# Decode attention, memory attention and retention of a hybrid layer computed in 32-wide tiles of the matmul array

## The chip, the core and the metric

One Trainium2 chip, one of its cores, one launch of one program. The metric is the device time of that launch in microseconds (us), the median over several runs; the profile is one further execution with the profiler on. Six units are named below: TensorE (PE for its matmuls, PEld for its weight loads), VectorE (DVE), ScalarE (ACT), GpSimd (POOL), SyncE (SP), which issues every transfer of this kernel, and the 16 DMA engines.

## The reference

One step of a layer with three gated branches. It is computed for a prompt of 2048 tokens and for 8 decode sequences of 16 new tokens each; "decode" below means the latter.

```python
h = rms_norm(x, g_norm);  z = h @ w_in                       # 1024 -> 9224
fq, fk, fv, ff, fg, rq, rk, rv, rg, mq, mg, gl = split_proj(z)
# A: 8 heads x 64; decode: 16 queries against 2048 cached keys and 16 new ones
s = q.k * 64**-0.5 + c_q - c_k;  p = softmax(s, causal);  fox_o = p @ v
# B: 4 heads, key width 128, value width 256; decode starts from a given state S
o     = (q @ S) * dec_q + ((q @ k.T) * dmask) @ v
S_new = gamma**L * S + (k * dec_k).T @ v
# M: 4 heads x 128 against 256 memory tokens
mem_o = softmax(mq @ mk.T * 128**-0.5) @ mv
y = x + (sum_i gate_i * (branch_i * silu(g_i)) @ w_p_i) @ w_out
```

All arrays are float32. The caches of A for decode hold 8 x 2048 x 512 keys and as many values.

## The kernel before, in words

The program has three stages. The first makes the projections for all tokens and stores them in DRAM (to about 1690 us). The second runs two lanes that a helper `weave` interleaves: the right lane does retention (prompt tiles, then `sample` for the decode sequences) and then `fox`, the prompt's attention of branch A; the left lane does the forget gates, `mem_prompt`, `decode_mem`, `decode_fox`, and then, when decode is finished and its buffers are given back, `out_block` for the first two token tiles (merge and output projection). The third stage is the other `out_block` calls. The order in which each engine gets its instructions is set when the program is built, by a scheduler that follows its own estimate of times; on the chip each engine then works through its list in that order.

Matmuls are written `T.matmul(out, stationary, moving)`. Type F32R is a reduced form, and a float32 value is split into two of them (`hi` and `lo`), with two or three matmuls; type F32 is used whole. In the trace a whole-F32 matmul shows as two weight loads and two matmuls, here called two passes, and an F32R matmul as one.

The steps that the change touches:

- `decode_fox`, `unit(b)`, one sequence. A column of the score bank `sc` (128 rows) is head group x 16 queries. `qblk` holds, for each of 4 head pairs `g`, a 128 x 128 stationary in which all columns but 32 are zero, so that four F32 matmuls of 128 columns over 512 keys add up in one bank (L1460); L1461 adds the forget term from 16 rows `crow`. A fifth, short chunk takes the 16 new keys (L1466 to L1468). Row maximum on DVE, exp on ACT; two units are in flight.
- Values: the probabilities are transposed (L1487) and split into hi and lo, which stand side by side as one 128-column stationary `dpr`; each value tile `dvt` is split too, by ACT (L1497, `dvh`) and POOL (L1499, `dvl`); then four F32R matmuls of 256 moving columns for each 128 keys (L1504). Only the blocks that belong to a head pair are used of the 128 x 512 result; L1520 sums hi and lo and transposes, by matmuls with `sumid`.
- `decode_mem`: the same with 4 heads, 64 columns and F32 (L1611, L1628, with transposes L1622 and L1635).
- `sample` in retention: for each of two head pairs and each sequence `b`, the states come in 256 KB loads `st0`, the queries of `b` are copied into a zeroed block `zq` (name qz), the keys are masked for `b` into `zk` (name kz); F32 matmuls L1188 (output) and L1189 (new state).
- `softmax_scale`, used by both `fox` and `decode_fox`: a subtraction on DVE and one exp on ACT (L1222, L1223).

Of the kernel before, what the change touches and what calls it, by code (L numbers as in the profile page):

```python
# [72 lines left out]
def body(ctx: ExitStack, tc: tile.TileContext, a, o, stop=99):  # L73
# [1019 lines left out]
    def retention(rp, rw):  # L1093
# [58 lines left out]
        def sample():  # L1152
# [7 lines left out]
            zq = rw.tile([P, 2, 2, P], F32, name="qz", bufs=1)  # L1160
            G.memset(zq, 0.0)
            yield
            ob = rw.tile([P, 4, 256], F32, name="ob", bufs=OB)
            for h2 in range(2):
# [5 lines left out]
                if h2:  # L1170
                    for b in (NB - 2, NB - 1):
                        G.memset(zq[:, b % 2, :, b * TS:(b + 1) * TS], 0.0)
                for b in range(NB):
                    bs = slice(b * TS, (b + 1) * TS)
                    s0 = rw.tile([P, 2, 256], F32, name="st0", bufs=3)
                    dma(s0, a["state_ret"][b][hs].rearrange("h k v -> k h v"))
                    zb = zq[:, b % 2]
                    if b >= 2:
                        G.memset(zb[:, :, (b - 2) * TS:(b - 1) * TS], 0.0)
                    G.tensor_copy(zb[:, :, bs], qt.rearrange("p (h l) -> p h l", h=4)[:, hs, bs])  # L1180
                    zk = rw.tile([P, 256], F32, name="kz")
                    G.tensor_scalar(zk, k[:, h2 * 256:(h2 + 1) * 256], kc[:, K_BM + b:K_BM + b + 1], 1.0, ALU.mult, ALU.mult)
                    up = prm()
                    sn = rw.tile([P, 2, 256], F32, name="sn0")
                    for i in range(2):
                        h = 2 * h2 + i
                        oc = slice(i * 256, (i + 1) * 256)
                        T.matmul(op[:, oc], zb[:, i], s0[:, i], start=False, stop=b == NB - 1 and i == 1)  # L1188
                        T.matmul(up[:, oc], zk[:, i * P:(i + 1) * P], v[:, h * 256:(h + 1) * 256], start=True, stop=True)  # L1189
                    for i in range(2):  # L1190
                        h = 2 * h2 + i
                        V.scalar_tensor_tensor(sn[:, i], s0[:, i], kc[:, K_GP + 4 + h:K_GP + 5 + h], up[:, i * 256:(i + 1) * 256], ALU.mult, ALU.add)
                    dma(o["ret_state_s"][b][hs].rearrange("h k v -> k h v"), sn)
                    yield
# [20 lines left out]
    def softmax_scale(nmx, l, f, nq, ncx, name):  # L1215
# [6 lines left out]
        V.tensor_tensor(f, nm.unsqueeze(2).broadcast_to([P, nq, ncx]), nmx, ALU.subtract)  # L1222
        S.activation(f, f, AF.Exp)  # L1223
# [145 lines left out]
    def decode_fox(dp, dw):  # L1369
# [53 lines left out]
        qblk = [dp.tile([P, 4, 160], F32, name=f"qb{i}") for i in range(2)]  # L1423
# [3 lines left out]
        def unit(b):  # L1427

            z = qblk[b % 2]
            for hf in range(2):  # L1430
                rr = slice(64 * hf, 64 * hf + 64)
                G.tensor_copy(z[rr, :, hf * TS:(hf + 1) * TS], qw[rr, :, b * TS:(b + 1) * TS])
            qb = z.rearrange("p g c -> p (g c)")[:, :512].rearrange("p (g c) -> p g c", g=4)
# [18 lines left out]
            for ci in range(5):  # L1452
                sc = pys()
                if ci < 4:
                    w = 512
                    for g2 in range(2):
                        kt = dw.tile([P, 2, 512], F32, name="dkt", bufs=4)
                        dma(kt, kv[:, 2 * g2:2 * g2 + 2, ci * 512:(ci + 1) * 512])
                        for g in range(2):
                            T.matmul(sc, qb[:, 2 * g2 + g], kt[:, g], start=g2 == 0 and g == 0, stop=False)  # L1460
                    T.matmul(sc, selr[32 * ci:32 * ci + 16], crow[32 * ci:32 * ci + 16], start=False, stop=True)  # L1461
                else:
                    w = 16
                    bs = slice(b * TS, (b + 1) * TS)
                    for g4 in range(4):
# [329 lines left out]
```

## Time and profile before

| | |
|---|---|
| runs, median (lowest to highest) | 3339.79 us (3335.1 to 3340.51), 3 runs |
| the profiled execution, and its span | 3333.96 us, 3331.8 us |
| PE / PEld busy | 3164.7 us (95%) / 2900.8 us (87%) |
| DVE / ACT / POOL busy | 2107.7 (63%) / 1655.8 (50%) / 981.8 us (29%) |
| granted TensorE clock, mean | 0.978 |
| bytes moved by DMA | 660.75 MB, mean 198 GB/s |

Busy is the union of an engine's instructions; matmuls overlap one another, and their ends are modelled. So how fast matmuls follow one another is read below from the starts of successive rows of the timeline, and not from the duration of one. In the trace the decode parts run between about 1879 us (retention) and 2683 us (the last store of `decode_fox`).

### The profile page before, as it was taken

Reading aid. Unit: us, or ns where it says so; the run is one execution under the profiler, and the core shown is the slowest. Engines: PE = TensorE matmul, PEld = TensorE weight load, DVE = VectorE, ACT = ScalarE, POOL = GpSimd, SP = SyncE. Lnnn points to the kernel's source line nnn. Section 1 sums busy time; section 2 is a strip of 40 time slices with the busy share of each in tenths; the row PEclk is TensorE's granted clock in tenths of the full one; section 3 lists DMA queues with packets and bytes.
Section 4 is the critical chain, followed back from the end, with each engine's and each line's share of the span. In section 5 each row is a group of like instructions: output and inputs, shape, how many; then the busy total and the mean of one; then the engine's idle time right before and its main releaser. Section 6 shows DMA issues by size and latency. Waiting matters only on the chain.

```text
span 3331.8 us, 57569 instructions
## 1 busy us (share of the span) xinstructions
PE 3164.7 (95%) x21243; PEld 2900.8 (87%) x21243; DVE 2107.7 (63%) x3478; ACT 1655.8 (50%) x3217; POOL 981.8 (29%) x917
## 2 busy tenths in 40 slices
PE   6999999999999999999979978999999999999999
PEld 5999999999999999999969945777777788889899
DVE  7777676756556566556667736766666886554444
ACT  4453444545445455445445635767677774222222
POOL 4446443100210020210011303666665853100100
PEclk8999999999999999999989988999999999999999
DMA  4776565677556658767677875555565458576665
GB/s 165 234 241 210 186 199 192 197 221 238 184 175 202 203 185 244 225 201 212 199 246 236 271 224 174 156 157 163 176 200 156 121 155 252 178 214 198 183 201 160
DMA packets 638445, 660.75 MB, mean 198 GB/s; under 512 B 46060, under 2 KB 553348, under 8 KB 638100
## 3 DMA queue, kind: packets, MB, share of 16 engines
q1 hardware_dynamic: 638164, 657.08, 63.9%
q8 instruction: 168, 2.75, 0.3%
q14 instruction: 113, 0.93, 0.1%
HBM read 477.52 MB, written 179.41 MB: 197 GB/s over the span
## 4 chain that ended last, share of the span: by engine, by line
PE 69%; DMA 11%; DVE 9%; issue 4%; ACT 4%; POOL 2%; SPq 1%; DVEq 0%; ACTq 0%; POOLq 0%
PE a L449 7%; PE a L451 7%; PE a L450 7%; PE b L449 5%; PE b L451 5%; PE b L450 5%; PE ys L1460 3%; PE ov L1344 3%; PE tp L1324 3%; DMA x<-in_x_prompt 2%; DMA out_y_p<-x 2%; DVE wl L400 2%; PE sc L1290 2%; PE ym L1504 2%; PE tp L227 1%
## 5 line engine op out<-in xcount | busy, mean ns | idle before, releaser
L400 DVE TENSOR_TENSOR wl<-wr,wh 128x1024 fp32r<-128x1024 f32 (+1 forms) x386 | 565.1, 1468 | 287.0 <-ACT wh L399 285.1
L399 ACT CAST wh<-wr 128x1024 fp32r<-128x1024 f32 (+1 forms) x386 | 404.6, 1050 | 306.8 <-PE b L451 128.2
L449 PE MATMUL a<-wh,ho 128*128 128x256 f32 (+1 forms) x1432 | 407.3, 285 | 14.7 <-ACT gz L707 8.4
L450 PE MATMUL a<-wl,ho 128*128 128x256 f32 (+1 forms) x1432 | 405.5, 283 | 5.8 <-DVE wl L400 5.8
L451 PE MATMUL a<-wh,ho 128*128 128x256 f32 (+1 forms) x1432 | 406.1, 284 | 0.7 <-DVE ho L276 0.7
L451 PE MATMUL b<-wh,ho 128*128 128x256 f32 (+1 forms) x1032 | 290.8, 282 | 5.4 <-DVE ho L276 5.4
L449 PE MATMUL b<-wh,ho 128*128 128x256 f32 (+1 forms) x1032 | 291.4, 283 | 4.3 <-ACT wh L399 2.3
L450 PE MATMUL b<-wl,ho 128*128 128x256 f32 (+1 forms) x1032 | 290.7, 282 | 0.6 <-DVE wl L400 0.6
L449 PEld LDWEIGHTS a<-wh,ho 128*128 128x128 f32 x1432 | 272.4, 190 | 18.3 <-ACT gz L707 10.4
L221 ACT CAST wh<-wraw 128x1024 fp32r<-128x1024 f32 x120 | 122.9, 1049 | 331.0 <-DMA wraw<-in_w_p 121.7
L428 POOL TENSOR_TENSOR wr<-wr 128x1024 f32<-128x1024 f32 (+1 forms) x72 | 200.1, 2779 | 272.1 <-DMA wr<-in_w_in 219.7
L450 PEld LDWEIGHTS a<-wl,ho 128*128 128x128 f32 x1432 | 272.6, 190 | 6.3 <-DVE wl L400 6.3
L451 PEld LDWEIGHTS a<-wh,ho 128*128 128x128 f32 x1432 | 272.6, 190 | 1.3 <-DVE ho L276 1.3
L449 PE MATMUL a<-ho,wh 128*128 128x384 f32 (+1 forms) x768 | 253.0, 329 | 1.8 <-ACT gz L707 1.7
L450 PE MATMUL a<-ho,wh 128*128 128x384 f32 (+1 forms) x768 | 253.3, 330 | 0.0
L451 PE MATMUL a<-ho,wl 128*128 128x384 f32 (+1 forms) x768 | 252.6, 330 | 0.0
L460 ACT COPY kp<-a 128x256 f32<-128x256 f32 (+3 forms) x384 | 152.9, 404 | 183.3 <-PE a L451 182.7
L1297 DVE TENSOR_REDUCE f_mx<-sc 128x1 f32<-128x512 f32 (+2 forms) x320 | 192.2, 604 | 66.1 <-PE sc L1293 33.1
L1302 POOL TENSOR_SCALAR pt<-pt,f_f,f_nm 128x512 f32<-128x512 f32 (+3 forms) x288 | 206.0, 730 | 93.8 <-DVE f_nm L1226 78.7
L1298 ACT ACTIVATE pt<-sc,f_mx 128x512 f32<-128x512 f32 (+2 forms) x320 | 200.8, 628 | 63.5 <-DVE f_mx L1297 55.7
L205 DVE TENSOR_TENSOR pl<-tp,ph 128x512 fp32r<-128x512 f32 (+2 forms) x352 | 193.0, 562 | 55.8 <-ACT ph L202 52.9
L451 PEld LDWEIGHTS b<-wh,ho 128*128 128x128 f32 x1032 | 195.1, 189 | 5.6 <-DVE ho L276 5.6
(375 smaller groups left out, 8819.0 us busy)
## 6 DMA issues: line engine op xcount, KB each, us to landing
wr<-in_w_in SPq DMA_DIRECT2D x170, 512.0 KB
wraw<-in_w_p SPq DMA_DIRECT2D x80, 512.0 KB
dkt<-in_cache_fox_k SPq DMA_DIRECT2D x64, 512.0 KB
dvt<-in_cache_fox_v SPq DMA_DIRECT2D x64, 512.0 KB
wr<-sum_gl SPq DMA_DIRECT2D x48, 512.0 KB
wraw<-in_w_out SPq DMA_DIRECT2D x40, 512.0 KB
gtd<-gz SPq DMA_DIRECT2D x96, 192.0 KB
gt<-gtd SPq DMA_DIRECT2D x24, 768.0 KB
```

The lines of the kernel that those rows point to most:

```text
L205: V.tensor_tensor(l, src, f32(h), ALU.subtract)
L221: S.copy(whv[:, i * hc:(i + 1) * hc], rv)
L399: S.copy(h, t)
L400: eng.tensor_tensor(l, t, f32(h), ALU.subtract)
L428: G.tensor_tensor(out, x, y, op)
L449: T.matmul(out, lh(c), rh(c), start=first and c == 0, stop=False, skip_group_check=True)
L450: T.matmul(out, lh(c), rl(c), start=False, stop=False, skip_group_check=True)
L451: T.matmul(out, ll(c), rh(c), start=False, stop=last and c == 3, skip_group_check=True)
L460: S.copy(t[nm], t["a"])
L1297: V.tensor_reduce(nmx[:, j, ci:ci + 1], sc[:, :w], AX.X, ALU.max, negate=True)
L1298: S.activation(pt[:, :w], sc[:, :w], AF.Exp, bias=nmx[:, j, ci:ci + 1], accum_out=l[:, j, ci:ci + 1])
L1302: G.tensor_scalar(pt, pt, fb, 0.5 if r is None else r[:, j:j + 1], ALU.mult, ALU.mult)
```

## The change

It uses a smaller part of the array for each decode matmul. With a stationary of 32 columns the result is written to 32 of the 128 rows of a bank, at rows 0, 32, 64 or 96, and four such matmuls in a row fill the bank.

- Scores of `decode_fox`: the zero columns go. The forget term comes first and opens the bank, then four F32 matmuls, each 32 columns by 512 keys, each into its own 32 rows.
- Values: no split any more of probabilities or values. The transposed probabilities are copied as F32; per 128 keys there are four F32 matmuls, each 32 columns by the 128 value columns of its head pair, into `ov[g, :P]`. `dvt` has 4 buffers, and `dvh`, `dvl`, their cast and subtraction are gone. The result is 128 x 128, and one transpose takes the place of the matmuls with `sumid`.
- `decode_mem`: the same with a head to each 32 rows; 128 x 128 transposes.
- `sample`: four sequences `2j + r` at a time, their output in 32-column tiles; the new state from 32 rows of `zk` and `v`, where a mask over pairs leaves the 16 rows of one sequence.
- `softmax_scale`: the subtraction becomes scale and bias of the exp, one ACT instruction per query tile.

```diff
 # sample
-            zq = rw.tile([P, 2, 2, P], F32, name="qz", bufs=1)
+            zq = rw.tile([P, 2, 4, 2, 32], F32, name="qz", bufs=1)
             G.memset(zq, 0.0)
+            qv = qt.rearrange("p (h j r t) -> p r j h t", h=4, j=4, r=2)
...
+            zk = rw.tile([P, 2, 512], F32, name="kz", bufs=1)
+            for r in range(2):
+                G.tensor_scalar(zk[:, r], k, bm[:, r:r + 1], 1.0, ALU.mult, ALU.mult)
...
-                        T.matmul(op[:, oc], zb[:, i], s0[:, i], start=False, stop=b == NB - 1 and i == 1)
-                        T.matmul(up[:, oc], zk[:, i * P:(i + 1) * P], v[:, h * 256:(h + 1) * 256], start=True, stop=True)
...
+                    for i in range(2):
+                        for j in range(4):
+                            T.matmul(op[32 * j:32 * j + 32, i * 256:(i + 1) * 256], zq[:, r, j, i], sts[j][:, i],
+                                     start=False, stop=r == 1 and i == 1)
...
+                            for j in (2 * j2, 2 * j2 + 1):
+                                g = slice(32 * j, 32 * j + 32)
+                                T.matmul(ups[j % 2][:, i * 256:(i + 1) * 256], zk[g, r, h * P:(h + 1) * P], v[g, h * 256:(h + 1) * 256],
+                                         start=True, stop=True)
 # softmax_scale
-        V.tensor_tensor(f, nm.unsqueeze(2).broadcast_to([P, nq, ncx]), nmx, ALU.subtract)
-        S.activation(f, f, AF.Exp)
+        for q in range(nq):
+            S.activation(f[:, q], nmx[:, q], AF.Exp, scale=-1.0, bias=nm[:, q:q + 1])
 # decode_fox
-        qblk = [dp.tile([P, 4, 160], F32, name=f"qb{i}") for i in range(2)]
+        qblk = [dp.tile([P, 4, 32], F32, name=f"qb{i}") for i in range(2)]
...
-                        for g in range(2):
-                            T.matmul(sc, qb[:, 2 * g2 + g], kt[:, g], start=g2 == 0 and g == 0, stop=False)
-                    T.matmul(sc, selr[32 * ci:32 * ci + 16], crow[32 * ci:32 * ci + 16], start=False, stop=True)
+                        kts += [kt[:, 0], kt[:, 1]]
+                    T.matmul(sc, selr[32 * ci:32 * ci + 16], crow[32 * ci:32 * ci + 16], start=True, stop=False)
+                    for g4 in range(4):
+                        T.matmul(sc[32 * g4:32 * g4 + 32], qb[:, g4], kts[g4], start=False, stop=True)
...
-                split(prv[:, :, 0], prv[:, :, 1], p[:rows, :n * P].rearrange("p (a c) -> p a c", c=64))
+                S.copy(pr[:rows, :n], p[:rows, :n * P].rearrange("p (j c) -> p j c", c=P))
...
-                            S.copy(vh, vt)
-                            for i in range(2):
-                                G.tensor_tensor(vl[:, i], vt[:, i], f32(vh)[:, i], ALU.subtract)
-                        for part in (vh, vl):
-                            for a2 in range(2):
-                                c = slice(a2 * 256, (a2 + 1) * 256)
-                                lt = pr[:, j, a2].rearrange("p r c -> p (r c)")
-                                T.matmul(ov[:, c], lt, part[:, j % 2, c], start=ci == 0 and j == 0 and a2 == 0 and part is vh, stop=False)
+                        for g4 in range(4):
+                            g = slice(32 * g4, 32 * g4 + 32)
+                            T.matmul(ov[g, :P], pr[:, j, g], vt[:, j % 2, g4 * P:(g4 + 1) * P], start=ci == 0 and j == 0, stop=False)
...
-            for g4 in range(4):
-                c0 = 96 * g4 - 32 * (g4 % 2)
-                T.matmul(p[:, c0:c0 + 64], os[:, g4 * P:(g4 + 1) * P], sumid, start=True, stop=True)
+            T.transpose(p[:, :P], os, ident)
 # decode_mem
-                T.matmul(sc[:64, :256], qb[:, h], kt[:, h], start=h == 0, stop=h == 3)
+                T.matmul(sc[32 * h:32 * h + 32, :256], qb[:, h], kt[:, h], start=True, stop=True)
...
-                T.matmul(ov[:64], pr[:, m], vt[:, m], start=m == 0, stop=m == 1)
+                for h in range(4):
+                    g = slice(32 * h, 32 * h + 32)
+                    T.matmul(ov[g, :P], pr[:, m, g], vt[:, m, h * P:(h + 1) * P], start=m == 0, stop=m == 1)
```

The order of instructions moves as well, since the scheduler estimates the new pieces anew. The lists below give line, operation, tiles and shape of the result. First, PE's list where a score chunk of `decode_fox` stands between matmuls of the prompt's attention. Before:

```order
L1290 MATMUL sc<-ka,qa 128x512
L1291 MATMUL sc<-kb,qb 128x512
L1460 MATMUL ys<-dkt,qb_22193 128x512 x4
L1461 MATMUL ys<-crow,selr 128x512
L1344 MATMUL ov<-ph,vv 128x256 x2
```

After the change:

```order
L1333 MATMUL tp<-kc,pt 128x128 x4
L1469 MATMUL ys<-crow,selr 128x512
L1472 MATMUL ys<-dkt,qb_22694 32x512 x4
L1353 MATMUL ov<-ph,vv 128x256 x2
L1299 MATMUL sc<-ka,qa 128x512
```

The four tile matmuls stand in a row, behind the 16-row matmul that stood behind them. Second, PE's list at the values of `decode_fox`. Before:

```order
L1504 MATMUL ym<-dvh,dpr 128x256 x2
L1504 MATMUL ym<-dvl,dpr 128x256 x2
L1504 MATMUL ym<-dvh,dpr 128x256 x2
L1504 MATMUL ym<-dvl,dpr 128x256 x2
L1504 MATMUL ym<-dvh,dpr 128x256 x2
L1504 MATMUL ym<-dvl,dpr 128x256 x2
L1504 MATMUL ym<-dvh,dpr 128x256 x2
L1504 MATMUL ym<-dvl,dpr 128x256 x2
```

After the change:

```order
L1353 MATMUL ov<-ph,vv 128x256 x2
L1353 MATMUL ov<-pl,vv 128x256 x2
L1508 MATMUL ym<-dvt,dpr 32x128 x16
L1333 MATMUL tp<-kc,pt 128x128 x4
L1353 MATMUL ov<-ph,vv 128x256 x2
```

Sixteen matmuls of 256 columns have become sixteen of 128, in one row of the list in 26 of the chunks. Third, SP's list of transfers where the first `out_block` begins: `iraw` is its input and `wraw` its weights; `qa`, `qb` and `fg` are loads of the prompt's attention, `ind<-f_ot` its stores, `ind<-doT` the last store of `decode_fox`. Before:

```order
L184 DMA ind<-doT 128x4x128
L184 DMA qa<-qtL 64x256
L184 DMA qb<-qtH 64x256
L184 DMA iraw<-ind 128x2x256
L184 DMA wraw<-in_w_p 128x8x128
L184 DMA iraw<-ind 128x2x256
L184 DMA wraw<-in_w_p 128x8x128
L184 DMA qb<-crq 4x256
```

After the change:

```order
L184 DMA ind<-f_ot 64x256
L184 DMA fg<-fgd 64x256
L184 DMA iraw<-ind 128x2x256
L184 DMA ind<-doT 128x4x128
L184 DMA iraw<-ind 128x2x256
L184 DMA wraw<-in_w_p 128x8x128 x2
L184 DMA iraw<-ind 128x2x256 x2
L184 DMA wraw<-in_w_p 128x8x128
```

Behind `doT` there were loads for further attention units (`qa`, `qb`); now there is none, and two stores are what is left of the prompt's attention. In PE's list the first `out_block` matmul came after 1045 of the 1152 value matmuls of `fox`, and comes now after 1128 of them.

More of the change, by code (lines that the diff above doesn't have):

```diff
@@ L1455, in unit @@
                     w = 512
+                    kts = []
                     for g2 in range(2):
@@ L1483, in unit @@
                 rows = P if ci < 4 else 16
-                pr = dw.tile([P, 4, 2, 2, 64], F32R, name="dpr", bufs=1)
+                pr = dw.tile([P, 4, P], F32, name="dpr")
                 for j in range(n):
                     T.transpose(p[:rows, j * P:(j + 1) * P], pts[ci][:, j * P:j * P + rows], ident)
-                prv = pr.rearrange("p j a r c -> p (j a) r c")[:rows, :2 * n]
-                split(prv[:, :, 0], prv[:, :, 1], p[:rows, :n * P].rearrange("p (a c) -> p a c", c=64))
+                S.copy(pr[:rows, :n], p[:rows, :n * P].rearrange("p (j c) -> p j c", c=P))
                 if ci < 4:
@@ L1507, in unit @@
                     dma(f32(vn), f32(vhl)[SEQ + b * TS:SEQ + (b + 1) * TS])
[L1508 to L1514 removed]
+                    vw = dw.tile([16, 8, 64], F32, name="dvw", bufs=1)
+                    V.tensor_tensor(vw, f32(vn)[:, :, 0:64], f32(vn)[:, :, 64:128], ALU.add)
+                    for g4 in range(4):
+                        g = slice(32 * g4, 32 * g4 + 32)
+                        T.matmul(ov[g, :P], pr[:16, 0, g], vw[:, 2 * g4:2 * g4 + 2].rearrange("p h d -> p (h d)"), start=False, stop=True)
+                    os = dw.tile([P, P], F32, name="dos", bufs=1)
+                    S.copy(os, ov[:, :P])
                 yield
             p = pdt()
[L1518 to L1521 removed]
+            T.transpose(p[:, :P], os, ident)
+            pv = p[:, :P].rearrange("p (g c) -> p g c", g=4)
             bs = slice(b * TS, (b + 1) * TS)
@@ L1592, in decode_mem @@
         V.tensor_tensor(qw, f32(qms[0]), f32(qms[1]), ALU.add)
-        qblk = [dp.tile([P, 4, 80], F32, name=f"mq{i}") for i in range(2)]
+        qblk = [dp.tile([P, 4, 32], F32, name=f"mq{i}") for i in range(2)]
         for z in qblk:
@@ L1621, in unit @@
             for m in range(2):
-                T.transpose(p[:, m * 64:(m + 1) * 64], pt[:, m * P:(m + 1) * P], ident[:64, :64])
-            pr = dw.tile([P, 2, 64], F32, name="mpr")
-            S.copy(pr, p[:, :128].rearrange("p (m c) -> p m c", m=2))
+                T.transpose(p[:, m * P:(m + 1) * P], pt[:, m * P:(m + 1) * P], ident)
+            pr = dw.tile([P, 2, P], F32, name="mpr")
+            S.copy(pr, p[:, :256].rearrange("p (m c) -> p m c", m=2))
             yield
```

89 lines of the change are left out of this document (37 added, 52 removed).

## The prediction

> **What bounds the kernel now.** I read the page first, for the busy shares and the chain of work that ended last:
>
> ```profile
> PE 3164.7 (95%) x21243; PEld 2900.8 (87%) x21243; DVE 2107.7 (63%) x3478; ACT 1655.8 (50%) x3217; POOL 981.8 (29%) x917
> PE 69%; DMA 11%; DVE 9%; issue 4%; ACT 4%; POOL 2%; SPq 1%; DVEq 0%; ACTq 0%; POOLq 0%
> ```
>
> TensorE is busy 95% of the span and is 69% of the chain. Then the stretches where the decode parts run (us from the start, then busy us and instructions for each engine, clock, DMA share, GB/s):
>
> ```profile
> 1890.00:2010.00 120.00, 97.30 (x492) 66.22 (x490) 55.92 (x175) 50.88 (x139) 23.93 (x63) 0.93 0.80 242
> 2010.00:2690.00 680.00, 641.34 (x3923) 499.61 (x3924) 474.71 (x1097) 478.10 (x1220) 425.57 (x527) 0.96 0.55 161
> 2690.00:2790.00 100.00, 92.11 (x717) 86.97 (x717) 83.28 (x131) 58.46 (x113) 56.85 (x49) 0.99 0.62 179
> ```
>
> In the 680 us of attention PE is idle for 39 us, DVE and ACT for about 200 each, DMA is at 0.55. So a PE microsecond saved there is nearly a microsecond of time. In the 120 us of retention's end and memory attention PE is idle for 23 us with DMA at 0.80, and one wait accounts for most of that:
>
> ```profile
> PE ys L1611 <- DMA mkt<-in_cache_mem_k: 14.3, 3, 8.4
> ```
>
> There only a part of what PE saves can show; I count half. The groups by line and shape (count, then busy us, mean ns) give what the decode parts run on PE:
>
> ```profile
> L1460 PE MATMUL ys<-dkt,qb 128*128 128x512 f32 x256 | 119.6, 610 | 1.6 <-ACT dpt L1471 0.8 <-POOL qb L1432 0.8
> L1504 PE MATMUL ym<-dvh,dpr 128*128 128x256 f32 x256 | 54.0, 293 | 3.8 <-DVE dpr L205 3.7
> L1504 PE MATMUL ym<-dvl,dpr 128*128 128x256 f32 x256 | 52.9, 288 | 0.0
> L1611 PE MATMUL ys<-mkt,mq 128*64 128x256 f32 x64 | 20.2, 480 | 14.4 <-DMA mkt<-in_cache_mem_k 14.3
> L1188 PE MATMUL ry<-st,qz 128*128 128x256 f32 x64 | 16.8, 383 | 0.8 <-DMA st<-in_state_ret 0.8
> L1189 PE MATMUL rm<-rv,kz 128*128 128x256 f32 x64 | 16.2, 381 | 0.5 <-DVE sn L1192 0.5
> L1628 PE MATMUL tp<-mvt,mpr 128*64 128x512 f32 x32 | 15.4, 604 | 0.7 <-ACT mpr L1624 0.7
> L1520 PE MATMUL tp<-sumid,dos 128*128 128x64 f32 x64 | 8.1, 271 | 0.0
> L1466 PE MATMUL ys<-dkw,qb 128*128 128x16 f32 x64 | 8.1, 254 | 0.0
> ```
>
> The code has 128 matmuls at L1460 and the trace 256: two passes each. Mean durations overlap, so I price a pass by the start of the next row. From the chain of waits, then from PE's timeline (start, us, line):
>
> ```profile
> 2115.68 3.44 PE ys L1460 x8
> ```
>
> ```profile
> 2115.52 3.60 PE L1460 MATMUL ys<-dkt,qb 128*128 128x512 f32 x8
> 2119.05 0.50 PE L1461 MATMUL ys<-crow,selr 16*128 16x512 f32 x1
> 2119.48 0.33 PE L1290 MATMUL sc<-ka,qa 128*128 128x128 f32 x1
> ...
> 2112.71 0.40 PE L1291 MATMUL sc<-kb,qb 68*128 68x512 f32 x1
> 2112.94 0.40 PE L1344 MATMUL ov<-ph,vv 128*128 128x256 f32 x2
> ...
> 2102.08 0.40 PE L1504 MATMUL ym<-dvh,dpr 128*128 128x256 f32 x2
> 2102.32 0.40 PE L1504 MATMUL ym<-dvl,dpr 128*128 128x256 f32 x2
> ...
> 2103.51 0.89 PE L1450 MATMUL tp<-identr,cb 128*16 128x128 f32 x12
> 2104.33 0.50 PE L1461 MATMUL ys<-crow,selr 16*128 16x512 f32 x1
> ...
> 2060.36 1.07 PE L1466 MATMUL ys<-dkw,qb 128*128 128x16 f32 x8
> 2061.36 0.27 PE L1467 MATMUL ys<-cnT,selr 16*128 16x16 f32 x1
> ...
> 1891.30 1.89 PE L1189 MATMUL rm<-rv,kz 128*128 128x256 f32 x8
> 1893.03 0.60 PE L1088 MATMUL tp<-kc,y 128*128 128x128 f32 x4
> ...
> 1977.03 1.93 PE L1628 MATMUL tp<-mvt,mpr 128*64 128x512 f32 x4 [0.16 <-ACT mpr L1624]
> 1978.89 0.33 PE L1622 MATMUL tp<-kc,mpt 64*128 64x64 f32 x2
> ```
>
> A pass of an F32 matmul over 512 columns takes 3.44 / 8 = 0.43 us, over 256 columns 1.73 / 8 = 0.217; that is 0.84 ns a column, so 128 columns would be 0.108. An F32R matmul over 256 takes 0.24 / 2 = 0.12. The quickest rows with a weight load for each matmul, L1450 with 16 columns, come every 0.82 / 12 = 0.068. A change of the shape of the array's part costs extra: eight L1460 take 3.53 to the 16-row L1461, 0.09 over 3.44; L1461 takes 0.43, and L1291, as long and without a change, 0.23, so 0.20 on leaving; four 64-column L1628 take 1.86 to L1622 against 4 x 0.43 = 1.72, 0.14.
>
> **The question no row answers** is whether matmuls in different columns run side by side: in this trace each has the array to itself. The lower bound for a group of four score matmuls is two passes (all four at once), 0.86 us; the upper is eight, 3.44, as now. I take five: rows start in the list's order, and the second pass of a matmul needs the same 32 columns as its first, so it waits; the first pass of the next tile, which stands behind it, can go with it. Then 1, 2, 2, 2, 1 passes are in the array, 5 x 0.43 = 2.15 us. It lies between the ends and needs nothing but the order of starts that all rows show.
>
> The Trainium skill, "TensorE: Matmul & The Clock Gate", Part 3, says that tiles in different columns run concurrently and that matmuls start and end in program order, and gives 2.38 times for three column tiles. It speaks of one pass a matmul; by its 2.38 the scores would take 46 us as an estimate, better than mine, and that is the second rival below. No run so far shows it.
>
> **Part by part,** on PE, in us:
>
> - Scores: 256 x 0.43 = 110; after, 32 chunks x 2.15 = 69: **-41**.
> - Short chunk: 64 x 1.00 / 8 = 8.0; after, 64 x 0.068 = 4.4: **-4**.
> - Values: 512 x 0.12 = 61. After, 512 F32 matmuls are 1024 passes of 128 columns: two at a time 0.054 each, but the quickest rows come every 0.068, so 1024 x 0.068 = 70: **+9**. Bounds: one at a time 0.108, 110 (+49), and 0.054, 55 (-6).
> - Sums: 8.1 busy for 64 L1520; after, 8 transposes of about 0.12: **-7**.
> - Fox switches of shape: in PE's list the changes of array part go from 136 to 322, of the 186 new ones 132 in `decode_fox`. At 0.10 (0.09 to 0.20): **+13**.
> - Retention: 128 passes x 0.217 = 28; after, with neighbours overlapping as far as the list keeps them together, about 20: **-8**. Memory: 64 x 0.217 + 32 x 0.43 = 28; after, 8 x 5 x 0.217 + 8 x 9 x 0.108 = 16.5: **-11**. The other 54 switches: **+5**. Together -14, half of it counted: **-7**.
>
> On the values the skill speaks against the change: "TensorEngine Tiling (Array Packing)", Instruction Overhead, warns of a fixed cost of about 60 cycles a matmul and against shortening what is short. The row says more than the page: 0.068 and not 60 cycles (0.025 us by the 2.4 GHz of "TensorE: Matmul & The Clock Gate", an estimate). By the page the values would cost 55 and the sum would be 15 better.
>
> The other engines lose work too:
>
> ```profile
> L1499 POOL TENSOR_TENSOR dvl<-dvt,dvh 128x512 fp32r<-128x512 f32 x128 | 160.5, 1279 | 76.9 <-PE ym L1504 43.8 <-ACT dvh L1497 27.3 <-PE ov L1344 2.8
> L1497 ACT CAST dvh<-dvt 128x1024 fp32r<-128x1024 f32 x64 | 66.5, 1045 | 23.4 <-DMA dvt<-in_cache_fox_v 10.4 <-PE ym L1504 6.2 <-issue 5.4
> L205 DVE TENSOR_TENSOR dpr<-tp,dpr 128x512 fp32r<-128x512 f32 (+1 forms) x40 | 24.1, 601 | 6.5 <-ACT dpr L202 6.4
> ```
>
> POOL loses 160, ACT 66, DVE 24. They are under cover of PE's 641 in those 680 us, so only what PE waits for them counts, and the largest such wait is
>
> ```profile
> PE sc L1290 <- ACT pt L1298: 19.9, 34, 2.8
> ```
>
> I take a quarter of it: **-5** (0 to -20). The exp with scale and bias (`softmax_scale`) swaps small DVE and ACT work under the same cover: 0. The 4 buffers of `dvt` and 6 of `st0` only let loads start earlier: 0.
>
> **What is late next** is the first `out_block`. It can't begin before `decode_fox` gives its buffers back, and its first inputs and weights took from 2692 to beyond 2709 to come in, in the chain of waits:
>
> ```profile
> 2692.12 0.97 ACT wh L221
> ...
> 2695.72 4.09 DMA wraw<-in_w_p
> ...
> 2705.30 4.20 DMA iraw<-ind
> ```
>
> Now attention of the prompt covers that: PE is 92% busy from 2690 to 2790. In the new list only 24 of the 1152 value matmuls of `fox` are left behind its start, not 107; 24 x 0.12 and their transposes are some 6 us. So of the 18 us to the last of those loads about 12 lie open: **+12** (0 to 30).
>
> Sum: `decode_fox` -41 - 4 + 9 - 7 + 13 = -30; with -7, -5 and +12 it is -30. The profiled execution, 3333.96 (span 3331.8), would become 3304; its time is 6 under the median of 3339.79, and the median would become **3310**.
>
> **Rivals.**
> 1. *One after another* (slower). If the array takes one matmul at a time also in tiles, the scores stay at 110, the values take 110 for 61, and the switches are still paid: fox 0 - 4 + 49 - 7 + 13 = +51, retention and memory +3, then -5 and +12: +61, **3401**. For it: no two matmuls of this trace share the array. Against it: that trace has no two in different columns. It decides as soon as a group of four scores takes over 3.3 us.
> 2. *All four at once.* Scores 32 x 0.86 = 27.5, -83; values still +9 by the 0.068; retention and memory about -32 with their switches, half counted: fox -72, -16, -5, +12: **3260**. For it: the skill's packing figures above. Against it: the two passes of one tile must follow each other, and the list is in order.
> 3. *Saved, but not seen*: the two units of `decode_fox` share one score bank, and DVE, ACT and PE pass it on in turn; if that round, and the open load of `out_block`, set the end, the time stays at about **3340**. For it: DVE's and ACT's 475 in 680. Against it: a round of 3.5 + 0.4 on PE and some 1.5 elsewhere, 40 times, is 220 of 680.
>
> **Chances.** Five passes 0.50, one after another 0.20, all at once 0.18, not seen 0.12. The likeliest one's own range, with switches at 0.2 and the load at 30 on one side, the load at 0 and -20 for waits on the other, is 3275 to 3340. The range for all reaches over most of rival 2 and a part of rival 1: 3245 to 3370. A difference under 0.2%, about 7 us, can't be told from none by these runs. Faster: 0.42 of the first, all of rival 2 and a third of rival 3: 0.64; same 0.11; slower 0.25.
>
> **What would show it.** In the timeline after, the start of four tile scores to the next row: 2.2 us (mine), 3.4 (rival 1), 0.9 (rival 2). Sixteen value matmuls: 2.2 us, against 3.4 if one at a time. The 16-row matmul 0.2 longer than its stream. PE idle where `out_block` begins, some 12 us more. Wrong would be a PE that stands idle among the tiles, waiting for weight loads, or a longer wait for DMA.

## The result, and the profile after

The changed kernel takes 3254.9 us (median; 3247.8 to 3264.71) against 3337.74 for the kernel before in the same session: a ratio of 0.975, with a 95% interval of 0.9732 to 0.9767. That is 83 us faster, where 30 were forecast. Direction and range held; the size did not.

The page of the changed kernel (its profiled execution took 3247.8 us), busy times of the engines and the chain that ended last:

```profile
span 3246.0 us, 58315 instructions
PE 3046.4 (94%) x21803; PEld 2798.0 (86%) x21803; DVE 2043.3 (63%) x3367; ACT 1603.4 (49%) x3201; POOL 816.3 (25%) x753
PE 70%; DMA 12%; DVE 7%; ACT 4%; issue 3%; POOL 2%; SPq 2%; DVEq 0%; ACTq 0%; POOLq 0%
```

TensorE is busy 118 us less (3164.7 to 3046.4), but the span is only 86 shorter: TensorE's idle time went from 167 to 200 us. So there are two questions: why TensorE saved so much, and where 33 us of it went.

The groups of TensorE by line and shape in the stage of the decode parts (count, then busy us and mean ns of one, then the idle time ahead):

```profile
L1472 PE MATMUL ys<-dkt,qb 128*32 128x512 f32 x256 | 44.3, 633 | 1.6 <-DMA dkt<-in_cache_fox_k 1.5
L1508 PE MATMUL ym<-dvt,dpr 128*32 128x128 f32 x1024 | 36.6, 276 | 0.6 <-ACT dpr L1499 0.6
L1194 PE MATMUL rm<-rv,kz 32*128 32x256 f32 x64 | 15.8, 400 | 0.4 <-DVE sn L1200 0.4
L1186 PE MATMUL ry<-st,qz 128*32 128x256 f32 x64 | 9.2, 388 | 0.1
L1613 PE MATMUL ys<-mkt,mq 128*32 128x256 f32 x64 | 7.3, 541 | 18.9 <-DMA mkt<-in_cache_mem_k 18.9
```

The scores went from 119.6 to 44.3 us, the values from 106.9 (two groups) to 36.6, memory's scores from 20.2 to 7.3. Retention's new states (16.2 to 15.8) gained nothing.

The timeline has the test that the prediction named. A group of four tile scores (eight passes), and a run of sixteen tile values (32 passes), each with the row behind it:

```profile
2311.30 0.50 PE L1469 MATMUL ys<-crow,selr 16*128 16x512 f32 x1
2311.73 1.07 PE L1472 MATMUL ys<-dkt,qb 128*32 128x512 f32 x8
2312.73 0.66 PE L1333 MATMUL tp<-kc,pt 128*128 128x128 f32 x4
...
2370.67 1.08 PE L1508 MATMUL ym<-dvt,dpr 128*32 128x128 f32 x32
2371.68 0.65 PE L1458 MATMUL tp<-identr,cb 128*16 128x128 f32 x8
```

From the start of four scores to the next row it is 1.00 us: not 2.2 (five passes), not 3.4 (one after another), but two passes of 0.43 and a change of shape. The trace's single records show how: the first passes of the four tiles start 7 ns apart, the four second passes 0.45 us later, again 7 ns apart. The sixteen values take 1.01 us, 0.032 for a pass; within the run four passes start together every 0.109 us, 0.027 for each.

Lastly the stretches of the stage (us from the start, then busy us and instructions of each engine, clock, DMA share, GB/s):

```profile
1890.00:2010.00 120.00, 88.62 (x595) 61.61 (x587) 64.74 (x175) 61.02 (x173) 25.23 (x50) 0.80 0.82 242
2010.00:2616.00 606.00, 554.41 (x4574) 427.03 (x4573) 429.41 (x1036) 435.01 (x1228) 274.73 (x408) 0.94 0.60 181
2616.00:2700.00 84.00, 68.33 (x484) 63.62 (x482) 60.40 (x84) 40.55 (x60) 40.38 (x27) 0.92 0.80 239
```

In the first of them PE is busy 88.62 of 120 (97.30 before) and the granted clock is 0.80 (0.93 before; over the whole execution it is 0.968 for 0.978). After the end of `decode_fox` at 2616 PE stands idle for 16 of 84 us. The lost 33 are spread: 9 more idle in the first stretch, 13 more in the attention that follows (52 of 606, for 39 of 680 before), and 9 more in the 84 us where the first output block begins (16, for 7 in the 84 us from 2690 in the kernel before).

### The profile page after: what moved, and what is told of

Same layout as the page of the kernel before. It is cut to its first block, busy times and chain, and to the rows that moved or that the text cites. A ratio compares the mean times of both kernels' runs of the same rounds, so it can differ in the third digit from the quotient of the medians.

```text
span 3246.0 us, 58315 instructions
## 1 busy us (share of the span) xinstructions
PE 3046.4 (94%) x21803; PEld 2798.0 (86%) x21803; DVE 2043.3 (63%) x3367; ACT 1603.4 (49%) x3201; POOL 816.3 (25%) x753
## 4 chain that ended last, share of the span: by engine, by line
PE 70%; DMA 12%; DVE 7%; ACT 4%; issue 3%; POOL 2%; SPq 2%; DVEq 0%; ACTq 0%; POOLq 0%
PE a L449 7%; PE a L451 7%; PE a L450 7%; PE b L449 5%; PE b L451 5%; PE b L450 5%; PE ov L1353 4%; PE tp L1333 3%; PE sc L1299 2%; SPq L184 2%; PE sc L1300 2%; DMA out_y_p<-x 2%; PE tp L227 1%; PE tp L226 1%; PE tp L228 1%
```

## The experiments

The theory after the result (A): all four tiles run side by side, in both passes, so the two passes over 512 columns count once and not four times. Its rivals: the prediction's own step (five passes), and that a 32-column matmul is quicker by itself. And for the loss: retention's part. Every time below stands against the kernel before in the same session.

**Each part alone.** Each kernel is the kernel before with one part of the change. The edits are pieces of the diff shown above; here is only what marks each:

```diff
 p_scores
+                        T.matmul(sc[32 * g4:32 * g4 + 32], qb[:, g4], kts[g4], start=False, stop=True)
 p_values
+                            T.matmul(ov[g, :P], pr[:, j, g], vt[:, j % 2, g4 * P:(g4 + 1) * P], ...)
 p_ret
+                            T.matmul(op[32 * j:32 * j + 32, i * 256:(i + 1) * 256], zq[:, r, j, i], sts[j][:, i], ...)
 p_mem
+                T.matmul(sc[32 * h:32 * h + 32, :256], qb[:, h], kt[:, h], start=True, stop=True)
 p_softmax
+            S.activation(f[:, q], nmx[:, q], AF.Exp, scale=-1.0, bias=nm[:, q:q + 1])
```

> The kernel before with one part of the change: fox decode's scores in four tiles of 32 columns; values, retention, memory attention and softmax scale stay as before. Theory A (the two passes of the four tiles both run side by side, 0.95 us to the next row's matmul for a group of four): 32 groups save about 70 us of TensorE starts, some 10 of it given back where the first output block loses its cover: 3265 to 3280 us. The prediction's step (five passes, 2.15 us for a group): about 41 saved, 3295 to 3305. One after another (3.4 us): 3335 to 3345.

> The kernel before with the tile values of fox decode alone (with the single copy of the weights and the one transpose at the end that go with them); the scores stay full width. Theory A (a pass of the values in 0.027 us, sixteen of them in 1.01 us): 31 us of starts and some 6 of the sums saved, 3300 to 3312 us. The prediction's step (a pass every 0.068 us): values +9, sums -7, half of the switches: 3335 to 3345. If it is the work taken off VectorE, ScalarE and GpSimd that paid, and not TensorE's, it is faster than TensorE's saving, under 3295.

> The kernel before with retention's decode alone in tiles (output by columns, new states by 32 rows). The prediction's step: 8 us of starts saved, half of it seen, 3330 to 3337. Theory B (this part sits where TensorE waits for loads, so its saving is not seen, and its loads by fours make the wait longer): 3337 to 3350.

> The kernel before with memory attention's decode alone in tiles of 32 columns. The prediction's step: 11 us of starts saved, half of it seen, 3329 to 3335. Theory B (its scores wait for the cache's loads, so nothing is seen): 3336 to 3341.

> The kernel before with the softmax scale alone (the exponent with scale and bias on ScalarE, without the subtraction on VectorE). The prediction's step: 0, 3332 to 3342. If VectorE's small work stands on the way to the score banks: 3320 to 3331.

| part alone | us | before | ratio (95%) | forecast for the part |
|---|---|---|---|---|
| p_scores | 3278.69 | 3341.69 | 0.9809 (0.9789 to 0.9829) | -41 |
| p_values | 3294.14 | 3341.69 | 0.9852 (0.9831 to 0.9874) | about +2, and some of the switches |
| p_ret | 3371.45 | 3341.69 | 1.0086 (1.0056 to 1.0115) | -4 (half of 8) |
| p_mem | 3342.12 | 3341.69 | 1.0003 (0.999 to 1.0017) | -5 (half of 11) |
| p_softmax | 3341.68 | 3338.64 | 1.0012 (0.9996 to 1.0028) | 0 |

The scores gave 63 and the values 48; softmax and memory gave nothing that can be measured; retention cost 30. On the scores theory A stands (3265 to 3280), and the five passes (3295 to 3305) fall. The values saved more than even A expected (3300 to 3312); their median lies just under the 3295 below which the expectation gives the rest to the other engines, and that is taken up further below. Their groups in the two kernels, alone:

```profile
L1463 PE MATMUL ys<-dkt,qb 128*32 128x512 f32 x256 | 38.9, 633 | 0.2 <-DMA dkt<-in_cache_fox_k 0.2
```

```profile
L1497 PE MATMUL ym<-dvt,dpr 128*32 128x128 f32 x1024 | 35.6, 276 | 0.2 <-ACT dpr L1488 0.2
```

The sum of the parts is 63 + 48 - 30 = 81, near the 83 of the whole. That the two agree so closely is partly chance: n_mem below, which has the scores, the values and softmax and nothing else, saves 93 and not 111, and memory's tiles, worth nothing alone, give 24 beside it.

**Do different columns make it?** The four score matmuls of a group all use the same 32 columns of the array, and so write the same 32 rows of the bank.

```diff
-                    T.matmul(sc, selr[32 * ci:32 * ci + 16], crow[32 * ci:32 * ci + 16], start=True, stop=False)
...
-                        T.matmul(sc[32 * g4:32 * g4 + 32], qb[:, g4], kts[g4], start=False, stop=True)
+                        T.matmul(sc[:32], qb[:, g4], kts[g4], start=g4 == 0, stop=g4 == 3)
+                    T.matmul(sc, selr[32 * ci:32 * ci + 16], crow[32 * ci:32 * ci + 16], start=True, stop=True)
```

The forget term moves behind the group and opens the whole bank, so this kernel leaves all scores of the cached keys out of its result, those of the first 32 rows too; the matmuls are run all the same.

> The changed kernel, but the four score matmuls of a group all write the first 32 columns of the array's part instead of four different ones (the scores of the rows 32 to 127 are left out); the same number of instructions of the same sizes, and the same changes of shape. Theory A (what saves the time is that different columns run side by side): the eight passes of a group follow each other, 3.4 us for 0.95, 32 times: 75 to 80 us slower than the changed kernel, 3320 to 3340 us. Theory B (a matmul with 32 columns is quicker by itself, or the shorter weight loads pay): within 15 us of the changed kernel, 3250 to 3270.

It took 3306.99 us (3304.3 to 3309.44), a ratio of 0.9903 (0.9879 to 0.9927): some 51 us slower than the changed kernel by the two ratios (0.0153 of 3337). Its timeline, its group of scores, and its stretch of attention:

```profile
2303.25 3.62 PE L1470 MATMUL ys<-dkt,qb 128*32 128x512 f32 x8
2306.80 0.50 PE L1299 MATMUL sc<-ka,qa 128*128 128x512 f32 x1
```

```profile
L1470 PE MATMUL ys<-dkt,qb 128*32 128x512 f32 x256 | 120.3, 611 | 8.7 <-POOL qb L1441 8.6
```

```profile
2010.00:2616.00 606.00, 564.31 (x4101) 392.81 (x4100) 388.40 (x942) 391.05 (x1108) 246.61 (x366) 0.96 0.58 174
```

The same eight passes take 3.55 us to the next row in place of 1.00, and the group 120.3 us, as much as at full width (119.6). So a 32-column matmul is no quicker by itself; only tiles in different columns, with their different rows of the bank, share the time. That is the mechanism, shown. The size was missed: the group is 76 us longer, and the time grew by 51, under the 75 to 80 expected. TensorE as a whole is busy 63 us more (3046.4 to 3109.0), 13 less than the group alone, at a mean granted clock of 0.972 for 0.968, and it is idle for 6 us less. The profiles show where: from the first decode score to the last it is 539 us for 458, the 80 expected, but the first score comes 16 us earlier (2046.3 for 2062.4). It no longer stands behind the forget term, whose first matmul starts at 2065.0 here and at 2061.6 in the changed kernel. In the stretch PE is idle 42 of 606 us where the changed kernel has 52. So this kernel moves more than the columns, and its 51 us show the direction, and the size only roughly.

**What retention's part costs.** `sample` had a `yield` after each of its 16 states; in the change it has one after each pair, 8 in all. The right lane counts these steps:

```
for _ in retention(*pools(s2, "right", ("rp", 1), ("rw", 2))):
    n += 1
    if n == 30:
        fox_first.update(q=load_q(f0, 1, 0, 0), k=load_k(f0, 0, 0))
    yield 245 / 36
```

Retention has 36 steps before and 28 after. So its lane has used 28 x 245 / 36 = 190 of the plan and not 245 when `fox` begins, `fox` is laid earlier against the left lane, and step 30, the early load of its first `q` and `k`, is never reached. In the trace the first value matmul of `fox` starts at 1958 us, for 1991 before. Four kernels take this apart: the steps given back in the changed kernel (y_two) and in the kernel with retention's part alone (pr_two), the early load alone (y_pre), the lane's count alone (y_pace).

```diff
 y_two, pr_two
                             dma(o["ret_state_s"][2 * j + r][hs].rearrange("h k v -> k h v"), sn)
                         yield
+                        yield
 y_pre
-                        if n == 30:
+                        if n == 22:
 y_pace
-                        yield 245 / 36
+                        yield 245 / 28
```

> The changed kernel with two yields instead of one after each pair of new states, so that retention again has 36 steps and not 28: its lane counts 245 units of the plan again and not 190, and the 30th step, at which fox's first q and k are loaded ahead, is reached again. Theory A (retention's part costs the kernel about 30 us because the 8 missing steps shift the lanes and drop that early load): 3210 to 3230 us, with 107 of fox's 1152 value matmuls behind the start of the first output block instead of 24, and without the 12 us waits for qa. Theory B (the tiles or the loads by fours of retention themselves cost it): 3248 to 3260, like the changed kernel.

> The kernel before with retention's decode in tiles alone, and two yields after each pair of new states (36 steps as before). Theory A (the missing steps): 3325 to 3340 us, so that the tiles of retention are worth nothing or a little. Theory B (the tiles or the loads by fours): 3360 to 3375, as with 28 steps.

> The changed kernel with fox's first q and k loaded at step 22 of 28 (so ahead again), the lanes shifted as in the changed kernel. If the missing early load is the larger part of the loss: 3215 to 3235 us; if the shift of the lanes (the lost cover of the first output block) is: 3240 to 3252.

> The changed kernel with a step of retention counted as 245/28 of the plan, so that its lane counts 245 again; the 30th step is still not reached, so fox's first q and k are not loaded ahead. If the shift of the lanes is the larger part of the loss: 3215 to 3235 us; if the missing early load is: 3240 to 3252.

| kernel | us | ratio (95%) |
|---|---|---|
| changed kernel | 3254.9 | 0.975 (0.9732 to 0.9767) |
| y_two | 3228.83 | 0.9658 (0.9632 to 0.9683) |
| y_pre | 3246.35 | 0.9714 (0.9689 to 0.974) |
| y_pace | 3242.17 | 0.97 (0.9672 to 0.9729) |
| pr_two | 3350.17 | 1.0031 (1.0017 to 1.0044) |

The eight lost steps cost the changed kernel 26 us by the medians (31 by the ratios), as theory A had it. The lane's count is the part that is resolved (its interval ends below the changed kernel's); the early load alone is not resolved from nothing. With retention alone about 18 of the 30 us come back (pr_two), and 10 to 12 stay: between the two theories, which each expected all or none. Where the 26 were, is seen in the changed kernel's stretches at the first output block, and then y_two's:

```profile
2580.00:2680.00 100.00, 86.30 (x652) 77.21 (x650) 75.35 (x131) 62.91 (x130) 47.89 (x46) 0.93 0.59 173
2680.00:2780.00 100.00, 90.64 (x511) 78.41 (x511) 50.99 (x60) 26.90 (x30) 22.30 (x13) 0.98 0.69 207
```

```profile
2580.00:2680.00 100.00, 92.40 (x722) 87.91 (x722) 78.88 (x128) 60.08 (x118) 57.22 (x50) 0.98 0.63 184
2680.00:2780.00 100.00, 99.18 (x459) 82.49 (x460) 54.69 (x65) 28.21 (x31) 13.23 (x9) 0.97 0.73 221
```

PE is idle 8 of these 200 us in place of 23: 15 of the 26. The other place is the start of `fox`. The waits of TensorE between 1890 and 2100 us in the changed kernel, in y_pre, and in y_pace (us in total, times, longest):

```profile
PE sc L1299 <- DMA qa<-qtL: 17.6, 2, 12.2
```

```profile
PE sc L1299 <- DMA qa<-qtL: 13.5, 2, 10.3
```

```profile
PE sc L1299 <- DMA qa<-qtL: 3.3, 2, 2.7
```

I had put this wait down to the missing early load. It stays when the load is given back (13.5) and goes when the lane's count is (3.3), without the load. So the wait belongs to the shift. The trace of the changed kernel shows behind what: the shorter of the two waits (5.4 us, to 1984) falls among the loads of memory attention, the last of which is issued at 2002; the longer (12.2, to 2046) does not. There SyncE issues the first loads of `decode_fox` from 2025 to 2041, with the DMA engines at 1.03 of their share from 2030 to 2040, and the `qa` that is waited for only at 2042, behind them. My reading of the early load falls; what it is worth beside the shift (y_two against y_pace, 13 us, with intervals that overlap) stays open.

**What is left of retention's tiles.** The changed kernel with retention taken back (m_ret), and with the tiles kept but the states loaded, used and stored one by one, 36 steps (r_seq):

```diff
 m_ret
-                for r in range(2):
...
+                for b in range(NB):
...
+                        T.matmul(op[:, oc], zb[:, i], s0[:, i], start=False, stop=b == NB - 1 and i == 1)
 r_seq
+                for b in range(NB):
+                    r, j = b % 2, b // 2
...
+                        T.matmul(op[g, oc], zq[:, r, j, i], s0[:, i], start=False, stop=r == 1 and i == 1)
```

> The changed kernel with retention's part taken back to what it was before (full width, loads one by one, 36 steps); fox decode and memory attention stay in tiles. If the parts add up, it is the changed kernel less what retention's part alone cost (30): 3218 to 3230 us. Against the changed kernel with 36 steps (3229) it shows retention's tiles without the steps: equal within 5 if they are worth nothing, 8 to 14 faster if they cost what they did alone with 36 steps (3350 against 3338).

> The changed kernel with retention's tiles kept, but states loaded, used and stored one by one in the old order and with the old 3 buffers, 36 steps. If the loads by fours cost the 8 us between the changed kernel with 36 steps (3229) and the one with retention as before (3221): 3217 to 3225. If the tiles themselves cost them (changes of the array's part): 3226 to 3235.

m_ret: 3221.37 us (3217.79 to 3228.08), 0.9649 (0.9624 to 0.9675), the best but for a kernel that can't be told from it, 3.5% faster than before and 1% faster than the changed kernel. r_seq: 3233.41, 0.9686 (0.9667 to 0.9706), no better than y_two (0.9658). So loads by fours are not what costs: without them it is not faster. (In r_seq outputs and new states also alternate, so that tiles can't run side by side; what that costs it is not separated.) Tiles in retention give nothing in any form tried here, and cost up to some 10 us; with 36 steps that cost is resolved only where the part stands alone (pr_two). The groups before and in p_ret, with the stretch of the kernel before ahead of them, suggest why so little is saved:

```profile
1890.00:1930.00 40.00, 37.97 (x241) 34.21 (x240) 25.33 (x65) 22.14 (x56) 14.22 (x41) 1.00 0.99 320
```

```profile
L1188 PE MATMUL ry<-st,qz 128*128 128x256 f32 x64 | 16.8, 383 | 0.8 <-DMA st<-in_state_ret 0.8
L1189 PE MATMUL rm<-rv,kz 128*128 128x256 f32 x64 | 16.2, 381 | 0.5 <-DVE sn L1192 0.5
```

```profile
L1194 PE MATMUL rm<-rv,kz 32*128 32x256 f32 x64 | 15.8, 400 | 0.4 <-DVE sn L1200 0.4
L1186 PE MATMUL ry<-st,qz 128*32 128x256 f32 x64 | 9.2, 388 | 0.0
```

The output (L1186) overlaps, for 7.6 us. Of the new states (L1194) few do: 8 of their 64 passes start within 30 ns of the pass ahead. All of this lies where DMA is at 0.99, and memory attention, which comes next, waits for its loads either way (14.3 us in the kernel before, 18.9 in the changed one); that this is why the 7.6 do not show is argued, not tested.

**Memory's tiles.** Alone they gave nothing. Beside the others (m_ret without them is n_mem) they should then give nothing too.

```diff
-                T.matmul(sc[32 * h:32 * h + 32, :256], qb[:, h], kt[:, h], start=True, stop=True)
+                T.matmul(sc[:64, :256], qb[:, h], kt[:, h], start=h == 0, stop=h == 3)
```

> The kernel before with fox decode's tiles and the softmax scale alone; retention and memory attention as before. If memory's tiles are worth nothing because that stretch waits for loads: 3215 to 3227, as with them (3221). If the 11 us of the prediction's step show beside the other tiles: 3228 to 3234. If the tiles cost there: under 3214.

n_mem took 3245.44 us (3243.38 to 3247.54), 0.9723 (0.9703 to 0.9743), 24 slower than m_ret: every theory missed it. The first decode score, in n_mem, in m_ret, in the kernel before and in p_mem:

```profile
2036.81 1.94 PE L1463 MATMUL ys<-dkt,qb 128*32 128x512 f32 x8
```

```profile
2024.85 1.94 PE L1463 MATMUL ys<-dkt,qb 128*32 128x512 f32 x8
```

```profile
2016.50 4.87 PE L1460 MATMUL ys<-dkt,qb 128*128 128x512 f32 x7 [0.81 <-POOL qb L1432]
```

```profile
2006.90 5.43 PE L1460 MATMUL ys<-dkt,qb 128*128 128x512 f32 x6
```

In both pairs memory's tiles bring `decode_fox` 10 to 12 us forward, so the 11 of the prediction's step is there. Alone, this lead is lost again in `decode_fox`: its last score comes at 2576.8 us in p_mem, for 2573.6 in the kernel before. Two stretches of p_mem, then of the kernel before:

```profile
2300.00:2400.00 100.00, 93.30 (x565) 75.53 (x565) 63.02 (x154) 68.05 (x180) 61.13 (x80) 0.91 0.52 160
2400.00:2500.00 100.00, 93.71 (x528) 68.53 (x528) 61.28 (x140) 67.42 (x167) 61.25 (x74) 0.97 0.65 185
```

```profile
2300.00:2400.00 100.00, 92.55 (x584) 74.25 (x584) 66.87 (x158) 69.74 (x182) 68.15 (x85) 0.97 0.54 162
2400.00:2500.00 100.00, 97.03 (x583) 73.15 (x584) 66.80 (x160) 73.99 (x190) 65.30 (x80) 0.98 0.68 195
```

The clock is lower by 0.06 in the first of these stretches and PE is busy 3.3 us less in the second, and it does 55 matmul instructions less in it. That is where most of the lead goes: the prompt's value matmul that starts at 2322 us in the kernel before comes 14.0 us earlier in p_mem, the one at 2491 only 4.6. In m_ret the lead of 12 over n_mem grows to 21 at the last decode score. Why it is lost in the one pair and grows in the other, no run settles.

**The other engines' work.** The values saved 48 us where TensorE is busy 33 less (3164.7 to 3131.8). Two kernels ask for the rest: v_work puts the old split of the loaded values back beside the tile values, for nothing; b_novl takes GpSimd's subtraction out of the kernel before, and with it the low part of the values out of its result.

```diff
 v_work (against p_values)
+                            vh = dw.tile([P, 2, 512], F32R, name="dvh")
+                            vl = dw.tile([P, 2, 512], F32R, name="dvl")
+                            S.copy(vh, vt)
+                            for i in range(2):
+                                G.tensor_tensor(vl[:, i], vt[:, i], f32(vh)[:, i], ALU.subtract)
 b_novl (against the kernel before)
-                            vl = dw.tile([P, 2, 512], F32R, name="dvl")
-                                G.tensor_tensor(vl[:, i], vt[:, i], f32(vh)[:, i], ALU.subtract)
-                        for part in (vh, vl):
+                        for n2, part in enumerate((vh, vh)):
```

> The kernel before with the tile values alone, as measured above (48 us saved, of which TensorE's busy time explains 33), and beside them ScalarE's copy and GpSimd's subtraction of the old split are run on the loaded values again, for nothing. If the 15 us beyond TensorE come from the work taken off ScalarE and GpSimd: 30 to 36 us saved, 3301 to 3309. If that work was under cover: as without it, 44 to 50 saved, 3288 to 3296.

> The kernel before, but GpSimd's subtraction for the low part of the values (128 of 1.28 us, 160 us) is gone and the matmuls of the low part read the high part again: the low part of the values is left out of the result, TensorE does the same work as before. If taking this work away is a part of what the tile values gain (15 of their 48 are more than TensorE's busy time): 3320 to 3330 us. If it was under cover of TensorE, as the prediction had it (5 for it and ScalarE's 66 together): 3333 to 3341.

v_work took 3363.74 us against 3338.64, 1.0071 (1.0051 to 1.009): slower than the kernel before, and outside both expectations. The waits of ScalarE at its copy between 2050 and 2690 us show one reason, first v_work, then the kernel before (its largest, and the one for the load):

```profile
ACT dvh L1497 <- DMA dvt<-in_cache_fox_v: 39.9, 27, 4.8
```

```profile
ACT dvh L1497 <- PE ym L1504: 6.2, 6, 3.6
ACT dvh L1497 <- DMA dvt<-in_cache_fox_v: 3.9, 5, 1.3
```

In v_work ScalarE stands at the copy until the load has landed, and the softmax of the prompt stands behind it; before, the load had mostly landed, and the longer wait was for a buffer. In the same stretch TensorE waits 25.6 us for the prompt's probabilities in v_work, for 12.6 in the kernel before, so this is a part of the loss and not all of it. v_work shows that this work is not under cover wherever it is put, but not what it cost before. b_novl does, for GpSimd's part: 3333.04 against 3339.45, 0.9981 (0.9971 to 0.9992), that is 6 us (3 to 10) for 160 us of GpSimd. The prediction's term for these waits (-5) had the right size. The 48 are then 33 of TensorE and 3 to 10 of GpSimd; the 5 to 12 that are left are about what the interval of the values (42 to 56) leaves open. What ScalarE's 66 us and VectorE's 24 were worth by themselves no run shows.

**Two attempts on the best version.** m_ret with the forget term as a matmul over all 128 rows (m_fullsel), which takes one change of shape out of each chunk, and m_ret with `decode_fox` laid closer (m_pace620).

```diff
 m_fullsel
-                    T.matmul(sc, selr[32 * ci:32 * ci + 16], crow[32 * ci:32 * ci + 16], start=True, stop=False)
+                    T.matmul(sc, selc[:, ci], crow, start=True, stop=False)
 m_pace620
-                yield from paced(decode_fox(*pools(st, "left", ("dp", 1), ("dw", 2))), 47, 730)
+                yield from paced(decode_fox(*pools(st, "left", ("dp", 1), ("dw", 2))), 47, 620)
```

> The changed kernel with retention as before, and the forget term of the scores as a matmul over all 128 rows with zeros in place of the matmul over 16 rows, so that one change of the array's part per chunk is gone: 32 times 0.2 us, 6 us less than the kernel with retention as before alone (3212 to 3224). If leaving a 16-row part costs nothing by itself: equal.

> The changed kernel with retention as before, and decode_fox spread over 620 of the plan instead of 730, so that 261 of the 1152 value matmuls of the prompt's attention are left behind the start of the first output block instead of 107. If loads of that block still stand open: 5 to 15 us less than the kernel with retention as before alone (3205 to 3220). If 107 cover them: equal, or slower by what the denser decode waits for its loads.

m_fullsel: 3218.84 us, 0.9643 (0.9619 to 0.9667), which can't be told from m_ret; the 6 us expected lie within the intervals. m_pace620: 3236.76, 0.969 (0.9662 to 0.9718), 15 slower by the medians. So with 261 matmuls left behind the output block's start in place of 107 it is no faster, and a denser `decode_fox` costs more than it hides.

## Why the prediction was wrong

The way and the wide range came out, and the account behind them did not: the five passes had their own range of 3275 to 3340, and 3254.9 lies below it. (By the terms that are named for it its lower end would be 3310 - 12 - 15 = 3283.) The wide range held because it reached over most of rival 2, to which it gave 0.18. Term by term:

- **Scores, -41.** The step that failed: "the second pass of a matmul needs the same 32 columns as its first, so it waits". The passes of four tiles do not take five rounds but two, all first ones together and then all second ones; the first pass of a tile starts ahead of the second pass of the tile before it: 0.86 us and the change of shape, not 2.15. Alone it is 63 us of time, 69 of TensorE (3164.7 to 3096.0). The lower bound that I named was the answer; rival 2's figure for it (27.5) leaves out the changes of shape and that the list splits some groups: from start to start the scores take 42 us (113 before).
- **Values, +9.** The step that failed is the floor of 0.068 us a pass, taken from rows whose matmuls all use the whole array: passes in four columns come every 0.027. From start to start the values took 65 us before and take 34 now: -31 in place of +9. The bound that I set, -6, did not hold it either, because I let only two passes go together. The Trainium skill's figure of about 60 cycles a matmul ("TensorEngine Tiling (Array Packing)", Instruction Overhead), 0.025 us as the prediction's estimate had it, lies close to the 0.027 measured, but no run shows that such a cost sets it: four passes every 0.109 us are what one stream of 128 columns takes at the prediction's 0.84 ns a column (0.108), and four tiles start within 0.02 us. I had gone by the row, and the row was of another kind of matmul.
- **Short chunk, -4, and sums, -7.** The groups went from 8.1 to 2.3 and from 8.1 to 2.3 us of busy time: -6 each, as far as busy time tells.
- **Switches, +13.** The size of one was right: two rounds of 0.43 are 0.86, and 1.00 to the next row leaves 0.14, within the 0.09 to 0.20. One fewer in each chunk (m_fullsel) can't be told from none.
- **Retention and memory, -7.** Half was counted. Measured alone: +30 and 0. The term for retention failed on something that the prediction did not look at: the number of steps in `sample`, which sets the plan's lanes. With the steps given back the part still cost 10 alone. For memory the 11 us are gained at the start of `decode_fox`, and alone they did not last to the end.
- **Waits, -5.** Right in size: b_novl gives 6 (3 to 10) for GpSimd's share.
- **Cover of the first output block, +12.** It was there (PE idle for 16 of the 84 us behind `decode_fox`; y_pace, which gives the cover back and also takes away most of the wait for `qa`, is 13 faster by the medians), but its cause was not a quicker `decode_fox`. In m_ret, where that is just as quick, 1045 matmuls stand ahead of the block as before. In y_two and y_pace, which give back the steps or their count, it is 1045 too. So that 24 were left and not 107 was the work of retention's missing steps.
- **The rivals.** One after another fell (1.00 us where it needed 3.3). All at once was right on the mechanism, and its 3260 is 5 from the result, but through errors that cancel: it kept the values at +9 where TensorE saved 31, and counted 16 as saved by retention and memory where, alone, retention lost 30 and memory gained nothing. Saved but not seen fell for the scores, and holds for memory's tiles alone.

## What to carry to other kernels

Price tiles in different columns of the array as one matmul for four, both passes of F32 too, as long as the list keeps them together; a floor read from full-width rows does not hold for them. Before a loop is rewritten in a program of generators, count its yields: where steps are the plan's clock or a trigger (`n == 30`), fewer of them move other work and drop loads, and nothing in the diff of the arithmetic shows it. A part that sits where the loads set the pace is measured alone and in company before its saving is counted: here memory's tiles gave 0 alone and 24 beside the others.

## What was not expected of the hardware

The granted clock falls where TensorE waits in memory attention, and it falls further with memory's tiles. The stretch in the kernel before, and in p_mem:

```profile
1930.00:2000.00 70.00, 50.65 (x203) 25.75 (x202) 22.19 (x86) 22.11 (x65) 5.25 (x15) 0.88 0.72 209
```

```profile
1930.00:2000.00 70.00, 39.75 (x329) 24.99 (x327) 28.89 (x87) 27.85 (x84) 11.06 (x24) 0.71 0.81 230
```

PE is busy 11 us less in it, and the clock is 0.71 for 0.88: 12 us of full clock less in 70 us. In the trace's record of the clock it is at half speed in one piece of 41 us there (p_mem), 37.5 (the changed kernel) and 44.4 (m_ret), with no piece over 10.2 us there in the kernel before and in n_mem, which has no tiles in memory attention. So in these traces a TensorE that does its work sooner and then waits for loads does a part of it at half the clock; that the waiting is what lowers the clock is not tested. The Trainium skill says the same in general, in "TensorE: Matmul & The Clock Gate", Part 1: the clock is gated down when the array has been idle for a window, and comes back with activity; the rows agree as far as they go.

The other is the 7 ns between the starts of matmuls in different columns. The Trainium skill has about 4 ns a tile in "TensorE: Matmul & The Clock Gate", Part 3; the trace has 7.
